# A decoder layer's recurrence: key transposes moved from TensorE to VectorE squares and transfers within SBUF

## The chip, the cores and the metric

One Trainium2 chip, one NeuronCore. The metric is the device time of the whole program in microseconds (us), the median of several runs.

## What is computed

A hybrid decoder layer on 256 tokens of width 2048, in float32. Its first part is a mixer with two branches, mLSTM and RWKV-7. The change touches the RWKV branch alone: 16 heads of size 64, a state matrix per head that goes from token to token.

```python
def step(state, inp):
    rt, wt, kt, vt, kkt, kat = inp
    state = (state * wt[:, :, None, :]
             - jnp.einsum('bhvk,bhk->bhv', state, kkt)[..., None] * kat[:, :, None, :]
             + vt[..., None] * kt[:, :, None, :])
    return state, jnp.einsum('bhvk,bhk->bhv', state, rt)
```

Around it stand projections by large weight matrices (some 350 MB of weights in all), cross-attention and a gated feed-forward.

## The kernel before, in words

Nearly all of TensorE's time goes to products of weights with activations. Each float32 product is made of three passes of a shorter float type: weight-high by activation-high, weight-high by activation-low and weight-low by activation-high. A weight comes from HBM in chunks of 512 KB (tile `raw`, four buffers; `Feed.dma`, line 384, issued on SP's queue at L392). ScalarE makes the high part (`wh`, L414) and VectorE the low part (`wl`, L458); both have four buffers. While TensorE works on chunk i, the program asks for the high and low parts up to chunk i+3 and for loads up to chunk i+6 (lines 545 and 546). A chunk is 24 matmuls of 256 columns (`fm`) or 12 of 512 (`tm`).

Everything else is woven between these products by `Spread` (line 71). Tasks are Python generators. `half()` runs at half-chunk steps, and a task with `chain=n` is given one piece (up to its next `yield`) every n such steps. `need(task)` runs a task to its end at once. This fixes the order in which each engine's instructions are written; each engine then works through its own list strictly in order, and waits at an instruction until what it reads is there and what it overwrites has been read. SP's queue is such a list too. The tile framework gives the queue's transfers eight completion semaphores in rotation, so a transfer can also wait for the one eight places ahead of it.

The RWKV recurrence (`rwkv`, line 1116, a chain task with a piece at every third step) works in four chunks of 64 tokens. `BK` holds the scaled keys with features on partitions, `[128, 8, 4, 2, 64]`: eight pairs of heads, four chunks, two kinds of key, 64 tokens. For chunk c it makes X, a two-level triangular solve (`lv1`, `lv2`), U, and, for chunks 0 to 2, the update `Tn` of the state. `Tn` needs the keys with tokens on partitions (`bkt`, in tile `bg`). `turn` (line 1155) makes them: TensorE transposes eight 128x128 squares per chunk into PSUM, two with `lv1`, two with `lv2` and four before U, and ScalarE copies them to `bg` (lines 1197, 1227 and 1250). The mLSTM branch (`mlstm`, line 1386) runs in the same stretch: products `den` and `num` on TensorE, then a chain of small steps over ScalarE (`rd`, `jk`), VectorE (`rd`, `var`, `rh`, `so`) and GpSimd (`rh`), for each of the two halves of the tokens.

The tile `gr2` `[128, 2, 1024]` has a second half that the solve of the inverses used (`L`, line 1036) and that is free once the recurrence begins.

Of the kernel before, what the change touches and what calls it, by code (L numbers as in the profile page):

```python
# [15 lines left out]
P = 128  # L16
# [129 lines left out]
def _layer(ctx, tc, nc, d, dbg):  # L146
    act, dve = Meter(nc.scalar, 200.0, 0.83), Meter(nc.vector, 70.0, 1.04)
    pool, pe, sp = nc.gpsimd, nc.tensor, nc.sync
    side = Spread(act, dve)
# [18 lines left out]
    def C(name, tag, shape=None, dt=F32):  # L168
        return mp.tile(shape or [P, S], dt, tag=tag, bufs=1, name=name)
# [7 lines left out]
    def aux(name, shape=None):  # L177
        return pp.tile(shape or [P, 512], F32, tag="aux", bufs=4, name=name)

    def mm(out, lhsT, rhs, start=True, stop=True):  # L180
        pe.matmul(out, lhsT, rhs, start=start, stop=stop, skip_group_check=True)  # L181
# [20 lines left out]
    def ccol(n, w, o=0):  # L202
        return con[:, CC[n] + o:CC[n] + o + w]

    ident = ccol("id", 128)
# [36 lines left out]
    def bc(ap, n):  # L242
        return ap.unsqueeze(1).broadcast_to((ap.shape[0], n, ap.shape[1]))
# [440 lines left out]
    M, tasks = {}, {}  # L684
# [424 lines left out]
            yield  # L1109


    T = [cp.tile([P, 4, 64], F32, name=f"T{hf}") for hf in range(2)]

    GAP = 3

    def rwkv():
        KR, BK, vt, cmt = M["KR"], M["BK"], M["vt"], M["cmt"]
        sm, im = ccol("sm", 64), ccol("im", 64)
        flat = lambda ap: ap.rearrange("p a t -> p (a t)")
# [2 lines left out]
        heads = [(hf, j, e) for hf in H for j in range(4) for e in H]  # L1122
        bg = C("bg", "bg0", [P, 2, 512])
        bkt = [bg[:, hf].rearrange("p (j t) -> p j t", j=4) for hf in H]
        gr = M["gr"]
        ab, uv = M["ab"], [v[:, 1] for v in M["au"]]
        m0, m1 = M["m0"], C("m", "m1", [P, 2, 4, 32])
# [4 lines left out]
        def gram(c, hf):  # L1132
            qs = [aux("gram", [P, 4, 128]) for _ in H]
            for j in range(4):
                for e in H:
                    mm(qs[e][:, j], flat(BK[E2[e], hf * 4 + j, c]), flat(KR[E2[e], hf * 4 + j, c]))

            def evac():
                for e in H:
                    dve.tensor_mul(ab[c][hf][:, e], qs[e][:, :, 0:64], bc(sm, 4))  # L1140
                    dve.tensor_mul(gr[hf][c % 2][:, e], qs[e][:, :, 64:128], bc(im, 4))
            return evac

        def early(c):
            def mask():
                for hf in H:
                    v = gr[hf][c].rearrange("p e j t -> p (e j) t")
                    nc.vector.tensor_mul(v, v, bc(im, 8))
                dve.spent += 1345.0
            return mask  # L1150
# [1 line left out]
        def booked():  # L1152
            dve.spent += 1345.0

        def turn(q, c, hf, js):
            for j in js:
                pe.transpose(q[:, j - js[0]], flat(BK[:, hf * 4 + j, c]), ident)

        def inverse(c, hf, k):
            return cmt[:, k, :, c * 8 + hf * 4:c * 8 + hf * 4 + 4].rearrange("p s j -> p j s")  # L1160

        def diagonal(c):
            for hf in H:
                dve.tensor_copy(m0[:, hf], inverse(c, hf, 0))
# [12 lines left out]
        def carried(c):  # L1177
            for hf in H:
                for e in H:
                    act.copy(ab[c][hf][E2[e], e], KR[E2[e], hf * 4:hf * 4 + 4, c, 0])  # L1180
                    act.copy(uv[hf][E2[e], e], T[hf][E2[e]])

        def quarter(name, c, js, more):
            q = aux(name, [P, 512])
            if more:
                turn(q[:, 256:512].rearrange("p (j t) -> p j t", j=2), c, 1, js)
            return q, q[:, 0:256].rearrange("p (h j s) -> p h j s", h=2, j=4)

        def level1(c, q, v, more):
            for hf, j, e in heads:  # L1190
                mm(v[quart[1][e], hf, j], ab[c][hf][quart[0][e], e, j, 32:64], m0[quart[0][e], hf, j])

            def evac():
                act.copy(m1[quart[1][0]], v[quart[1][0]])
                dve.tensor_copy(m1[quart[1][1]], v[quart[1][1]])
                if more:
                    act.copy(flat(bkt[1][:, 0:2]), q[:, 256:512])
            return evac

        dve.spent += 350.0  # L1200
        transposed(0)
        values(0)
        yield
        level1(0, *quarter("lv1", 0, (0, 1), True), True)()
        yield
        for c in range(4):
            more = c < 3

            if c % 2 == 0:
                ysb = [C(f"ysb{hf}", f"ysb{hf}", [P, 8, 64]) for hf in H]  # L1210
            q, v = quarter("lv2", c, (2, 3), more)
            x = aux("X", [P, 2, 4, 64])
            for hf, j, e in heads:
                r = slice(0, P) if c else E2[1 - e]
                mm(x[E2[e], hf, j], ab[c][hf][r, e, j], uv[hf][r, e, j])
            ev = []
            if more:
                ev.append(gram(c + 1, 0) if c == 2 else booked if c else early(0))
            for hf, j, e in heads:
                mm(v[quart[0][e], hf, j], m1[quart[1][e], hf, j], mt[hf][quart[1][e], j, 32:64])  # L1220
            for hf in H:
                for e in H:
                    r = quart[0][e]
                    dve.tensor_copy(mt[hf][r, :, 32:64], v[r, hf])
                    act.copy(uv[hf][E2[e], e], x[E2[e], hf])
            if more:
                act.copy(flat(bkt[1][:, 2:4]), q[:, 256:512])
            for f in ev:
                f()
            yield  # L1230
            if more:
                diagonal(c + 1)
            yield

            if c == 2:
                yield from turned(0, ysb_done)
                yield
            q = aux("U", [P, 2, 4, 64])
            ev = []
            if more:  # L1240
                qb = aux("bkt", [P, 4, 128])
                turn(qb, c, 0, (0, 1, 2, 3))
                ev.append(gram(c + 1, 1) if c == 2 else booked if c else early(1))
            for hf, j, e in heads:
                mm(q[E2[e], hf, j], mt[hf][E2[e], j], uv[hf][E2[e], e, j])
            for hf in H:
                act.copy(uv[hf][E2[0], 0], q[E2[0], hf])
                dve.tensor_copy(uv[hf][E2[1], 1], q[E2[1], hf])
            if more:
                act.copy(bkt[0], qb)  # L1250
            for f in ev:
                f()
            yield
            if more:
                transposed(c + 1)
            yield

            if more:
                lv1 = quarter("lv1", c + 1, (0, 1), c + 1 < 3)
                q = aux("Tn", [P, 2, 4, 64])  # L1260
                for hf, j, e in heads:
                    mm(q[E2[e], hf, j], bkt[hf][:, j, e * 64:e * 64 + 64], uv[hf][:, e, j])
            qy = aux("Y", [P, 2, 4, 64])
            for hf, j, e in heads:
                mm(qy[E2[e], hf, j], gr[hf][c % 2][:, e, j], uv[hf][:, e, j], start=(hf == 0 and j == 0), stop=(c == 0))
            if c:
                for hf, j, e in heads:
                    mm(qy[E2[e], hf, j], KR[E2[e], hf * 4 + j, c, 1], T[hf][E2[e], j], start=False)
            f = level1(c + 1, *lv1, c + 1 < 3) if more else None
            if more:  # L1270
                for hf in H:
                    pcb = pce[:, hf * 4:hf * 4 + 4, c].unsqueeze(2).broadcast_to((P, 4, 64))
                    if c:
                        dve.tensor_add(T[hf], T[hf], q[:, hf])
                        dve.tensor_mul(T[hf], T[hf], pcb)
                    else:
                        dve.tensor_mul(T[hf], q[:, hf], pcb)
            cr = E2[c % 2]
            for hf in H:
                ye = ysb[hf].rearrange("p (a b) v -> p b a v", b=2)  # L1280
                for e in H:
                    act.copy(ye[cr, e], qy[E2[e], hf])
            if c == 0:
                for hf in H:
                    nc.vector.tensor_mul(gr[hf][0].rearrange("p e j t -> p (e j) t"),
                                         M["gr2"][:, 0, hf * 512:hf * 512 + 512].rearrange("p (a t) -> p a t", a=8), bc(im, 8))
            if f:
                f()
            yield
            if more:  # L1290
                values(c + 1)
                yield
                carried(c + 1)
            yield
            if c % 2:
                ysb_done = ysb
                yield from norm(ysb, [gr[hf][1].rearrange("p e j t -> p (e j) t") for hf in H])
# [798 lines left out]
def _ptile(v):  # L2096
    return np.ascontiguousarray(v.reshape(-1, P).T)

# [83 lines left out]
```

## Time and profile before

| | |
|---|---|
| median of 3 runs | 1858.66 us (1858.31 to 1858.88) |
| profiled execution, its own time | 1858.71 us |
| span of the profile, first to last instruction | 1856.9 us |
| TensorE busy | 1848.2 us, 100% of the span |
| VectorE, ScalarE, GpSimd busy | 70%, 55%, 2% |
| chain of work that ended last, TensorE's share | 96% |

The span is 1.8 us shorter than the execution's own time. A busy share is the time in which at least one instruction of an engine runs; matmuls overlap, so TensorE at 100% says that it is never left without work, not that it works at its peak. The chain is followed back from the last instruction to whatever released it; its shares say which engine's work the end waited for. The recurrence lies between 295 and 475 us from the span's start.

### The profile page before, as it was taken

To read this page: it belongs to the slowest core of one execution; us is meant where nothing else is said; L and a number is where in the kernel's file an instruction comes from. 1 tells how busy PE (TensorE), PEld (TensorE's weight loads), DVE (VectorE), ACT (ScalarE), POOL (GpSimd) and SP (SyncE) were. 2 spreads that over 40 slices of the span, in tenths; PEclk is the share of its full clock that TensorE was granted. 3 is DMA by queue.
4 is the path that set the end of the run, shared out by engine and by line. 5 is a ranking of instruction groups with operands and counts; after the bars stand their busy time and mean duration, and the time that the engine had idled before them with its cause. 6 is when DMAs were issued, how large, how long until landed. Compare 5 with 4: busy or idle time off the path is not lost.

```text
span 1856.9 us, 36219 instructions
## 1 busy us (share of the span) xinstructions
PE 1848.2 (100%) x14902; PEld 1763.8 (95%) x14902; DVE 1302.8 (70%) x1857; ACT 1013.1 (55%) x1492; POOL 35.2 (2%) x64
## 2 busy tenths in 40 slices
PE   9999999999999999999999999999999999999998
PEld 9999888999999999999999999999999988888887
DVE  7789787566676857787876677766666775556565
ACT  7776445655454746666544555444445554555544
POOL 0100020000000000000000000000000000000000
PEclk9999999999999999999999999999999999999999
DMA  8556544455556765455776666666666666666664
GB/s 276 182 175 194 181 152 161 131 166 155 178 193 196 272 203 181 163 178 180 214 226 200 194 197 187 193 197 197 196 193 194 193 194 216 192 193 193 194 192 145
DMA packets 100454, 353.56 MB, mean 190 GB/s; under 512 B 11520, under 2 KB 12800, under 8 KB 99904
## 3 DMA queue, kind: packets, MB, share of 16 engines
q1 hardware_dynamic: 99712, 350.33, 59.8%
q8 instruction: 116, 1.90, 0.4%
q10 hardware_dynamic: 576, 0.92, 0.2%
q14 instruction: 50, 0.41, 0.1%
HBM read 347.01 MB, written 2.10 MB: 188 GB/s over the span
## 4 chain that ended last, share of the span: by engine, by line
PE 96%; DVE 1%; DMA 1%; ACT 0%; issue 0%; SPq 0%; DVEq 0%; ACTq 0%
PE fm L181 67%; PE tm L181 25%; DMA w<-in_w_in_dram 1%; DVE wl L458 0%; PE gram L181 0%; PE Y L181 0%; PE num L181 0%; PE lv L181 0%; DVE ql L66 0%; PE X L181 0%; PE U L181 0%; PE zg L181 0%; PE zwa L181 0%; DVE z L66 0%; DVE stx L66 0%
## 5 line engine op out<-in xcount | busy, mean ns | idle before, releaser
L458 DVE TENSOR_TENSOR wl<-raw,wh 128x1024 fp32r<-128x1024 f32 x639 | 775.4, 1218 | 405.6 <-ACT wh L414 401.2
L414 ACT CAST wh<-raw 128x1024 fp32r<-128x1024 f32 x639 | 664.6, 1045 | 485.7 <-PE fm L181 371.7
L181 PE MATMUL fm<-fh,wh 128*128 128x256 f32 x2048 | 563.8, 276 | 0.6 <-DVE fh L66 0.6
L181 PE MATMUL fm<-fh,wl 128*128 128x256 f32 x2048 | 563.5, 276 | 0.0
L181 PE MATMUL fm<-fl,wh 128*128 128x256 f32 x2048 | 563.4, 276 | 0.0
L181 PEld LDWEIGHTS fm<-fh,wh 128*128 128x128 f32 x2048 | 383.7, 188 | 0.8 <-DVE fh L66 0.8
L181 PEld LDWEIGHTS fm<-fl,wh 128*128 128x128 f32 x2048 | 383.6, 188 | 0.0
L181 PEld LDWEIGHTS fm<-fh,wl 128*128 128x128 f32 x2048 | 383.6, 188 | 0.0
L181 PE MATMUL tm<-wh,as 128*128 128x512 f32 x1024 | 315.2, 389 | 0.0
L181 PE MATMUL fm<-hh,wh 128*128 128x256 f32 x1024 | 283.8, 279 | 0.0
L181 PE MATMUL fm<-hh,wl 128*128 128x256 f32 x1024 | 281.5, 277 | 0.0
L181 PE MATMUL fm<-hl,wh 128*128 128x256 f32 x1024 | 281.3, 277 | 0.0
L181 PEld LDWEIGHTS tm<-wh,as 128*128 128x128 f32 x1024 | 192.1, 188 | 39.7
L181 PE MATMUL tm<-wl,as 128*128 128x512 f32 x512 | 199.2, 389 | 0.0
L181 PEld LDWEIGHTS fm<-hh,wh 128*128 128x128 f32 x1024 | 192.1, 188 | 0.7 <-ACT hh L66 0.2
L181 PEld LDWEIGHTS fm<-hl,wh 128*128 128x128 f32 x1024 | 191.5, 188 | 0.1
L181 PEld LDWEIGHTS fm<-hh,wl 128*128 128x128 f32 x1024 | 191.4, 188 | 0.0
L181 PEld LDWEIGHTS tm<-wl,as 128*128 128x128 f32 x512 | 96.1, 188 | 20.2
L66 ACT CAST as<-ac 128x256 fp32r<-128x256 f32 x128 | 45.6, 404 | 110.8 <-PE tm L181 110.8
L66 DVE TENSOR_TENSOR as<-ac,as 128x256 fp32r<-128x256 f32 x128 | 48.5, 421 | 61.7 <-ACT as L66 61.7
L181 PE MATMUL fm<-mgh,wh 128*128 128x256 f32 x256 | 70.9, 277 | 0.0
L181 PE MATMUL fm<-mgl,wh 128*128 128x256 f32 x256 | 70.8, 276 | 0.0
(417 smaller groups left out, 2218.9 us busy)
## 6 DMA issues: line engine op xcount, KB each, us to landing
raw<-in_w_fu_dram SPq DMA_DIRECT2D x256, 512.0 KB, 4.2
raw<-in_w_in_dram SPq DMA_DIRECT2D x154, 512.0 KB, 3.6
raw<-in_w_fd_dram SPq DMA_DIRECT2D x128, 512.0 KB, 3.9
raw<-in_w_br_dram SPq DMA_DIRECT2D x32, 512.0 KB, 3.9
raw<-in_w_mo_dram SPq DMA_DIRECT2D x32, 512.0 KB, 3.9
raw<-in_w_xk_dram SPq DMA_DIRECT2D x8, 512.0 KB, 4.2
raw<-in_w_xv_dram SPq DMA_DIRECT2D x8, 512.0 KB, 3.6
raw<-in_w_xq_dram SPq DMA_DIRECT2D x8, 512.0 KB, 3.8
```

The lines of the kernel that those rows point to most:

```text
L66: return f(out, *a, **k)
L181: pe.matmul(out, lhsT, rhs, start=start, stop=stop, skip_group_check=True)
L414: nc.scalar.copy(wh[:, v], r[:, v])
L458: nc.vector.tensor_sub(wl[:, v], r[:, v], self.st[self.nl][0][:, v])
```

## The change

A new chain task, `keys_turn`, gets the keys of chunks 0, 1 and 2 into token order inside `BK` itself. Per chunk VectorE transposes 32x32 squares, with two instructions of 128x512 elements, from `BK` into the free half of `gr2`. Then 16 transfers on SP's queue, each 32 partitions by 2 rows of 512 bytes, carry the squares to their places over `BK`'s chunk. The task is given a piece at every half-chunk step (`chain=1`), whatever the engines' budgets (`free=True`), and `need(tasks["keys"])` writes out what is left of it before U of chunk 0. The 24 TensorE transposes go. ScalarE's copies to `bg` stay, with the same number of elements, but read `BK` in SBUF. The planner's budgets are booked as if nothing had changed.

```diff
+    def keys_turn():
+        sq = M["gr2"][:, 1].rearrange("p (q k e) -> p k q e", q=4, k=8)
+        for c in range(3):
+            v = M["BK"][:, :, c].rearrange("p k b t -> p k (b t)")
+            for h in range(2):
+                h4 = slice(h * 4, h * 4 + 4)
+                nc.vector.transpose(sq[:, h4], v[:, h4].rearrange("p k (q s) -> p k q s", q=4))
+                yield
+            yield
+            for q in range(4):
+                for f in range(4):
+                    sp.dma_start(v[q * 32:q * 32 + 32, f * 2:f * 2 + 2],
+                                 M["gr2"][f * 32:f * 32 + 32, 1, q * 256:q * 256 + 256].rearrange("p (h i) -> p h i", h=2))
+            yield
...
+        tasks["keys"] = side.add(keys_turn(), chain=1, free=True)
...
-        def turn(q, c, hf, js):
-            for j in js:
-                pe.transpose(q[:, j - js[0]], flat(BK[:, hf * 4 + j, c]), ident)
+        def turn(c, hf, js):
+            src = BK[:, :, c].rearrange("p (f h) b t -> p h f (b t)", h=2)[:, hf]
+            src = src.rearrange("p f (j w) -> p j f w", j=4)
+            act.copy(bkt[hf][:, js].rearrange("p j (f w) -> p j f w", f=4), src[:, js])
...
+            if c == 0:
+                side.need(tasks["keys"])
...
-                qb = aux("bkt", [P, 4, 128])
-                turn(qb, c, 0, (0, 1, 2, 3))
...
-                act.copy(bkt[0], qb)
+                turn(c, 0, slice(0, 4))
+                if c == 0:
+                    turn(c, 1, slice(0, 4))
```

In the order of instructions three places matter. First VectorE's list at chunk 0 of the recurrence. Before, the low weight parts (`wl`) and the copies out of `lv1` and `lv2` (to `m` and `mt`) follow one another:

```order
L66 TENSOR_TENSOR mt_3575<-cmt_3004,con_73 128x256 [waits DVE_49]
L66 TENSOR_TENSOR mt_3576<-cmt_3004,con_73 128x256
L458 TENSOR_TENSOR wl_3591<-raw_3529,wh_3589 128x2x512 [waits DMAHW4_49,PE_49,Activation_49]
L66 COPY m_3574<-lv1_3607 32x256 [waits Activation_49]
L458 TENSOR_TENSOR wl_3631<-raw_3547,wh_3629 128x1024 [waits DMAHW5_49,DVE_49,Activation_49]
L458 TENSOR_TENSOR wl_3649<-raw_3565,wh_3647 128x1024 [waits DVE_49,DMAHW6_49,PE_49,Activation_49]
L66 COPY mt_3575<-lv2_3661 32x4x32 [waits DVE_49,PE_49]
```

After the change, the part of the list from the first transpose of key chunk 1 to `pws`, the first step of the mLSTM's second half (`DMAHW0` to `DMAHW7` are the eight semaphores of SP's transfers):

```order
L1118 STREAM_TRANSPOSE gr2_3119<-BK_1316 128x4x4x32 [waits DMAHW4_49,DMAHW3_49,DMAHW5_49,DMAHW2_49,DMAHW6_49,DMAHW1_49,DMAHW7_49,DMAHW0_49,DVE_49]
L458 TENSOR_TENSOR wl_3665<-raw_3565,wh_3663 128x1024 [waits PE_49,Activation_49]
L66 COPY mt_3575<-lv2_3677 32x4x32 [waits PE_49]
L66 COPY mt_3575<-lv2_3677 32x4x32
L66 COPY mt_3576<-lv2_3677 32x4x32 x2
L1164 TENSOR_TENSOR gx_2996<-gx_2996,con_73 128x512
L1164 TENSOR_TENSOR gx_2997<-gx_2997,con_73 128x512
L1118 STREAM_TRANSPOSE gr2_3119<-BK_1316 128x4x4x32 [waits DVE_49]
L458 TENSOR_TENSOR wl_3732<-raw_3594,wh_3730 128x1024 [waits PE_49,Activation_49]
L66 COPY m_3521<-cmt_3004 128x128 x2
L1118 STREAM_TRANSPOSE gr2_3119<-BK_1316 128x4x4x32 [waits DMAHW4_49,DMAHW3_49,DMAHW5_49,DMAHW2_49,DMAHW6_49,DMAHW1_49,DMAHW7_49,DMAHW0_49,DVE_49]
L1118 STREAM_TRANSPOSE gr2_3119<-BK_1316 128x4x4x32 [waits DVE_49]
```

Six transposes came in; the third and the fifth wait for all transfers of the chunk before, since they overwrite the squares that these read, and `wl`, `mt` and later `pws` stand behind them.

Second, SP's list in the same stretch, as the difference between the two:

```order
-L392 DMA raw<-in_w_in_dram 128x1024 x103
+L392 DMA raw<-in_w_in_dram 128x1024 x92
+L1123 DMA BK<-gr_3119 32x2x128 x16
+L392 DMA raw<-in_w_in_dram 128x1024 x2
+L1123 DMA BK<-gr_3119 32x2x128 x32
+L392 DMA raw<-in_w_in_dram 128x1024 x9
```

Between 92 and 103 weight loads 48 transfers of keys came in, with two weight loads between the first 16 and the other 32.

Third, TensorE at `lv1` of chunk 0, as the difference:

```order
 L181 MATMUL tm<-wl,hh 128x512
-L1157 MATMUL lv_3607<-con,BK 128x128 x2
-L181 MATMUL lv_3607<-m,ab 32x32 x16
+L181 MATMUL lv_3609<-m,ab 32x32 x16
 L181 MATMUL tm<-wh,hh 128x512
```

The two transposes are gone and nothing else moved.

## Rows read from the trace of the kernel before

**Rows 1.** The page: busy time and share of each engine; the chain's shares by engine.
```profile
PE 1848.2 (100%) x14902; PEld 1763.8 (95%) x14902; DVE 1302.8 (70%) x1857; ACT 1013.1 (55%) x1492; POOL 35.2 (2%) x64
...
PE 96%; DVE 1%; DMA 1%; ACT 0%; issue 0%; SPq 0%; DVEq 0%; ACTq 0%
```

**Rows 2.** Windows: stretch, length, PE, PEld, DVE, ACT, POOL busy; PE clock, DMA share, GB/s.
```profile
295.00:328.00 33.00, 33.00 (x317) 29.73 (x317) 21.39 (x38) 17.16 (x38) 1.02 (x1) 1.00 0.49 161
...
1850.00:1857.00 7.00, 1.29 (x5) 0.68 (x4) 2.67 (x4) 1.66 (x6) 0.00 (x0) 0.87 0.54 201
```

**Rows 3.** Chain of work that ended last, in order of time: start, us, what.
```profile
299.99 0.22 PE lv L1157 x2
...
318.30 0.44 PE bkt L1157 x4
...
340.64 9.63 PE fm L181 x84
```

**Rows 4.** The transposes' line, L1157: count, duration ns min/median/max, first and last start.
```profile
L1157 PE MATMUL lv<-con,BK x12: 270/272/273, 299.8 to 404.3; 128*128 128x128 f32 x12
...
L1157 PE MATMUL bkt<-con,BK x12: 270/272/273, 318.1 to 425.0; 128*128 128x128 f32 x12
```

**Rows 5.** Timeline of PE, 318 to 329 us: start, us, what.
```profile
318.14 0.60 PE L1157 MATMUL bkt<-con,BK 128*128 128x128 f32 x4
318.67 1.15 PE L181 MATMUL U<-au,mt 64*64 64x64 f32 x32
...
323.96 0.95 PE L181 MATMUL den<-ones,pws 128*128 128x1 f32 x8
324.76 3.70 PE L181 MATMUL num<-vm,pw 128*128 128x256 f32 x16
328.11 0.47 PE L181 MATMUL fm<-hh,wh 128*128 128x256 f32 x1
```

**Rows 6.** VectorE's transposes of squares, groups by line: busy us, mean ns of one.
```profile
L1063 DVE STREAM_TRANSPOSE cmt<-gr 128x1024 f32<-128x1024 f32 x1 | 2.1, 2108 | 0.0
...
L66 DVE STREAM_TRANSPOSE cmt<-gr 128x1024 f32<-128x1024 f32 x1 | 1.2, 1233 | 0.0
...
L1994 DVE STREAM_TRANSPOSE xsq<-xr 128x256 f32<-128x256 f32 x16 | 7.0, 437 | 0.0
```

**Rows 7.** Timeline of SP's queue near 900 us: four transfers within SBUF, then a weight load.
```profile
901.48 2.46 SPq L1997 DMA_DIRECT2D xt<-xsq  x4
904.04 6.67 SPq L392 DMA_DIRECT2D raw<-in_w_fu_dram  x4
```

**Rows 8.** Line L1997, transfers within SBUF: issue ns min/median/max, and time to landing.
```profile
L1997 SPq DMA_DIRECT2D xt<-xsq x32: 512/586/674, 901.5 to 978.1; - x32
...
DMA to landing us min/median/max: 2.5/3.7/4.5
```

**Rows 9.** Line L392, weight loads: issue ns min/median/max, and time to landing.
```profile
L392 SPq DMA_DIRECT2D raw<-in_w_in_dram x154: 327/328/1102, 14.1 to 573.9; - x154
...
DMA to landing us min/median/max: 2.7/4.0/11.4
```

**Rows 10.** SP's own waits, 285 to 340 us: us in total, times, longest.
```profile
SPq L392 <- DVE wl L458: 43.6, 12, 9.1
```

**Rows 11.** Timeline of VectorE, 297 to 319 us.
```profile
297.41 1.16 DVE L66 TENSOR_TENSOR mt<-cmt,con 128x256 f32<-128x256 f32 x2
298.50 1.21 DVE L458 TENSOR_TENSOR wl<-raw,wh 128x1024 fp32r<-128x1024 f32 x1
...
307.13 1.18 DVE L66 COPY mt<-lv 32x128 f32<-32x128 f32 x4 [1.17 <-PE lv L181]
308.34 1.29 DVE L1148 TENSOR_TENSOR gx<-gx,con 128x512 f32<-128x512 f32 x2
...
311.30 0.68 DVE L66 TENSOR_TENSOR pws<-pw 128x512 f32<-128x512 f32 x1
...
316.70 1.66 DVE L66 SCALAR_TENSOR_TENSOR so<-num,rh,so 128x256 f32<-128x256 f32 x4
```

**Rows 12.** Timeline of ScalarE: the first `jk` of the mLSTM's first half.
```profile
313.23 0.47 ACT L66 ACTIVATE jk<-num,rd 128x256 f32<-128x256 f32 x1 [0.80 <-PE num L181]
```

More of the change, by code (lines that the diff above doesn't have):

```diff
@@ L1181, in carried, with quarter, level1 @@
                     act.copy(uv[hf][E2[e], e], T[hf][E2[e]])
[L1183 to L1189, printed above, removed]
+        def quarter(name):
+            return aux(name, [P, 2, 4, 32])
+        def level1(c, v, more):
             for hf, j, e in heads:
@@ L1195, in evac @@
                 dve.tensor_copy(m1[quart[1][1]], v[quart[1][1]])
-                if more:
-                    act.copy(flat(bkt[1][:, 0:2]), q[:, 256:512])
+                if more and c:
+                    turn(c, 1, slice(0, 2))
+                elif more:
+                    act.spent += act.fixed + act.per * 256
             return evac
@@ L1203, in rwkv @@
         yield
-        level1(0, *quarter("lv1", 0, (0, 1), True), True)()
+        level1(0, quarter("lv1"), True)()
         yield
@@ L1210, in rwkv @@
                 ysb = [C(f"ysb{hf}", f"ysb{hf}", [P, 8, 64]) for hf in H]
-            q, v = quarter("lv2", c, (2, 3), more)
+            v = quarter("lv2")
             x = aux("X", [P, 2, 4, 64])
@@ L1225, in rwkv @@
                     act.copy(uv[hf][E2[e], e], x[E2[e], hf])
-            if more:
-                act.copy(flat(bkt[1][:, 2:4]), q[:, 256:512])
+            if more and c:
+                turn(c, 1, slice(2, 4))
+            elif more:
+                act.spent += act.fixed + act.per * 256
             for f in ev:
@@ L1258, in rwkv @@
             if more:
-                lv1 = quarter("lv1", c + 1, (0, 1), c + 1 < 3)
+                lv1 = quarter("lv1")
                 q = aux("Tn", [P, 2, 4, 64])
@@ L1268, in rwkv @@
                     mm(qy[E2[e], hf, j], KR[E2[e], hf * 4 + j, c, 1], T[hf][E2[e], j], start=False)
-            f = level1(c + 1, *lv1, c + 1 < 3) if more else None
+            f = level1(c + 1, lv1, c + 1 < 3) if more else None
             if more:
```

## The prediction

> **What bounds the kernel now.** I read the page's busy shares first, then its chain. TensorE is busy for the whole span and 96% of the chain is TensorE's work, while VectorE has 30% idle [rows 1]. The same holds where the change acts: from 295 to 328 us TensorE is busy for all 33 us, VectorE for 21.4 and ScalarE for 17.2, and the transfer engines are half used [rows 2]. So an instruction taken from TensorE shortens the run by what it occupies there, and work added on VectorE or on SP's queue is free as long as nothing that TensorE reads comes late through it. The question is therefore what stands behind the new waits in those two lists.
>
> **What the removal gives.** 24 transposes go, 12 with `lv` and 12 for `bkt` [rows 4]. Each is 272 ns long but overlaps the next: the chain gives 0.22 us to two and 0.44 to four [rows 3], 0.11 each, so 24 x 0.11 = 2.64 us. From start to start four of them and the step to U take 0.53 us [rows 5], which would make 24 x 0.13 = 3.2 us; that is the upper end. I take 2.64, all of it on the path. ScalarE's copies keep their element count and only change their source; ScalarE is idle half the time here [rows 2], so I cost them at nothing. The lost cover would be a ScalarE that is late with `wh`.
>
> **What a chunk's 16 transfers take.** The nearest rows are the transfers within SBUF near 900 us, also 32 partitions each. Four are issued in 2.46 us and the next load starts 2.56 us after the first [rows 7], 0.64 us from one to the next; one lands 3.7 us after its issue [rows 8]. So from the first issue to the last landing I put b = 15 x 0.64 + 3.7 = 13.3 us. The low end takes the issue of a weight load, 0.33 us [rows 9], and the quickest landing, 2.5 [rows 8]: 15 x 0.33 + 2.5 = 7.5. The high end takes the longest issue, 0.67 [rows 8], with the same gap of 0.05, and the slowest landing, 4.5: 15 x 0.72 + 4.5 = 15.3. I stay with 13.3, since those rows are of the same kind of transfer, from the same queue, in a row.
>
> [...] The rows have 0.64 in a series. [...]
>
> **The new waits, step by step.** A new transpose has 512 elements: twice the 437 ns of the 256-element ones [rows 6] is 0.87 us, with 0.62 and 1.05 (half of the two 1024-element ones) as ends. Times are on the clock of the profile of before.
> - VectorE is through with `mt` at 298.5 [rows 11]. Transpose 0a, one `wl` of 1.21, transpose 0b: 301.45. Then SP issues chunk 0's transfers, landed at 301.45 + b = 314.75.
> - Transpose 1a overwrites the squares that these transfers read, so VectorE stands still at it until then, and behind it `wl` (1.21), the `mt` copies (1.18), `gx` (1.29) [rows 11], then 1b: 0.87 + 1.21 + 1.18 + 1.29 + 0.87 = 5.42 more, so 306.87 + b = 320.2. In the profile before, U, which needs these `mt`, starts at 318.67 [rows 5] and `mt` was ready at 308.3; now it is ready at 318.0 on a TensorE that is by then 0.9 us earlier (8 transposes). That is at its limit; a wait of about a microsecond here vanishes in the longer one that follows.
> - SP issues chunk 1's transfers after 1b; they land at 306.87 + 2b = 333.5. Transposes 2a and 2b, one after the other, wait for that: 308.61 + 2b = 335.2.
> - Behind them stands `pws`, which `den` of the mLSTM's second half reads. TensorE came to `den` at 323.96 [rows 5], so here it stands from about 323 on. After `pws` come `rd`, ScalarE's `jk`, `var`, GpSimd's power, `rh` and `so`. From `pws` to the end of `so` took 311.30 to 318.36 [rows 11], 7.06 us, with some 0.9 us in it in which `jk` waited for TensorE's `num` [rows 12]; without that 6.2. The second `num` reuses the PSUM that `so` reads and needs half of the four `so`: 5.5 us after 2b. `num` then takes 324.76 to 328.11, 3.35 us [rows 5].
> - So `num` ends at 308.61 + 2b + 5.5 + 3.35 = 317.46 + 2b, where it ended at 328.11: 2b - 10.65 later. The other 16 transposes give 1.76 back afterwards. **Net: 2b - 12.4 = +14.2 us** at b = 13.3, +2.6 at 7.5, +18.2 at 15.3.
>
> The weights do not add to it. `wl` of the next chunks follows `so` while `num` runs. The first weight load behind all 48 transfers goes out at 335.2 + 16 x 0.64 = 345.4, lands 4.0 us later [rows 9], and is ready after a cast and a subtraction of some 2.3 us at 351.7. TensorE reads it at 340.64 [rows 3] plus 15.7, the shift at that point, at 356.3. The added VectorE work itself, 6 x 0.87 = 5.2 us, fits in its idle time. Chunk 2's transfers are first read a chunk of the recurrence later.
>
> **The clock.** TensorE would stand for over 10 us with little between. [...] I put 2 us, with 0 and 4 as ends. [...]
>
> **The sum.** The profiled execution took 1858.71 us (its span 1856.9 and 1.8 around it), 0.05 from the median of the runs. 1858.7 + 14.2 + 2 = 1874.9, so **1875 us**.
>
> **The rivals.**
> - *The transfers are quick enough, and the run is not slower.* Net is zero loss, -2.64, where 2b - 12.4 = -2.64, so for b of 4.9 us or less: 1856.1 us (1855.5 at the upper end of the removal). For it speaks only that 16 transfers of 32 KB are as many bytes as one weight load; against it that even at the issue of a weight load, 0.33 us each, 15 issues take 5 us before the last begins to move. Between 4.9 and 8 us the loss and the gain are within 3.7 us of each other, at about 1859: this is the case at the low end of b.
> - *SP's queue starves the weights.* SP issues in order; its own waits here, 43.6 us for `wl` [rows 10], are what a full queue of weights looks like. With 32 key transfers and no load between them, a pace p per issue delays the first load to 308.61 + 2b + 16p, and ready to 6.3 us after it, against a need at 340.64 + 2b - 10.65 - 0.2: it decides from p = 0.93 us on. If the two rows of 512 bytes per partition make an issue cost twice, p = 1.28: b = 22.9, net +33.4, then 5.6 for weights and 2 for the clock: 1900 us.
>
> **How the numbers follow.** A measurement of this kernel can tell about 0.2%, 3.7 us, from no change. The forecast's mechanism with b between 8 and 15.3 us: 0.82. The low end of b, within 0.2% of before: 0.08. Quick transfers: 0.03, of which a third beyond 0.2% if waits of the old run go too. Starved weights or an issue still longer: 0.07. So faster 0.02, same 0.09, slower 0.89. The range goes from b = 7.5 without a clock loss, 1861, less 1 for shorter transposes, to b = 15.3 with 4 us of clock, 1881, plus 1 for longer ones: 1860 to 1882.
>
> **What would show it.** In the profile of the changed kernel: no line of transposes on TensorE; two waits of VectorE at the new transposes, of about 10 us each, released by transfers; TensorE idle by some 10 us before `den` and again before `num` near 324 to 341, and busy elsewhere; 16 issues in about 10 us on SP's queue, three times; a granted clock below 1.00 after the gap. Wrong would be: a TensorE that stays at 100% near 330 us (then b is under 8), transfers that land as one batch within 5 us, or idle time of TensorE that ends at `wl` or `wh` for weights that landed late.

## The result and the profile after

The changed kernel takes 1874.63 us (median of 4 runs, 1874.29 to 1875.12) against 1858.49 of the kernel before on the same chip: a ratio of 1.0087, 95% interval 1.0071 to 1.0103. It is 16.1 us slower; the forecast was 1875. The profiled execution took 1874.46 us with a span of 1872.6.

The page of the changed kernel, busy shares and the shares of the chain that ended last:

```profile
PE 1850.2 (99%) x14878; PEld 1765.2 (94%) x14878; DVE 1306.7 (70%) x1863; ACT 1013.3 (54%) x1491; POOL 35.2 (2%) x64
...
PE 98%; SPq 1%; DVE 1%; ACT 0%; issue 0%; DMA 0%; POOL 0%; DVEq 0%; ACTq 0%; POOLq 0%
```

Against [rows 1] TensorE has 24 instructions less and VectorE 6 more, and 1% of the chain now lies on SP's queue, all of it between 320 and 340 us. Windows of that stretch (columns as in [rows 2]):

```profile
295.00:328.00 33.00, 28.01 (x285) 24.93 (x283) 13.65 (x21) 9.12 (x17) 0.00 (x0) 0.98 0.42 125
328.00:345.00 17.00, 9.35 (x46) 8.47 (x47) 10.12 (x19) 6.52 (x16) 1.02 (x1) 0.63 0.22 57
345.00:360.00 15.00, 13.35 (x190) 13.05 (x189) 10.57 (x22) 10.88 (x26) 1.01 (x1) 1.00 0.62 226
```

TensorE was busy for all of the first stretch before [rows 2]; now it is idle for 5.0, 7.65 and 1.65 us of the three, 14.3 in all, and its mean granted clock is 0.63 in the second. What it waits for stands in its timeline (start, us, what, idle time before and what ended it):

```profile
332.76 1.86 PE L181 MATMUL den<-ones,pws 128*128 128x1 f32 x8 [9.75 <-DVE pws L66]
337.51 5.19 PE L181 MATMUL num<-vm,pw 128*128 128x256 f32 x16 [2.88 <-DVE so L66]
346.76 1.15 PE L181 MATMUL Tn<-au,bg 128*64 128x64 f32 x32
350.50 0.69 PE L181 MATMUL lv<-m,ab 32*32 32x32 f32 x32 [1.65 <-DVE so L66]
...
355.33 1.04 PE L1449 MATMUL haT<-con,so 128*128 128x128 f32 x8
```

In the kernel before `Tn` and `lv` started at:

```profile
332.75 1.15 PE L181 MATMUL Tn<-au,bg 128*64 128x64 f32 x32
334.77 0.69 PE L181 MATMUL lv<-m,ab 32*32 32x32 f32 x32
```

Each time it is VectorE that is late, with `pws`, with `so` of the mLSTM's first half and with `so` of its second half (`lv` is the first level of the solve for the recurrence's chunk 1). VectorE's timeline says why:

```profile
298.17 0.71 DVE L1118 STREAM_TRANSPOSE gr<-BK 128x512 f32<-128x512 f32 x1
299.90 0.71 DVE L1118 STREAM_TRANSPOSE gr<-BK 128x512 f32<-128x512 f32 x1
312.97 0.71 DVE L1118 STREAM_TRANSPOSE gr<-BK 128x512 f32<-128x512 f32 x1 [9.95 <-DMA BK<-gr]
317.29 0.71 DVE L1118 STREAM_TRANSPOSE gr<-BK 128x512 f32<-128x512 f32 x1
330.83 1.31 DVE L1118 STREAM_TRANSPOSE gr<-BK 128x512 f32<-128x512 f32 x2 [11.32 <-DMA BK<-gr]
332.06 0.65 DVE L66 TENSOR_TENSOR pws<-pw 128x512 f32<-128x512 f32 x1
336.58 1.66 DVE L66 SCALAR_TENSOR_TENSOR so<-num,rh,so 128x256 f32<-128x256 f32 x4
349.56 1.66 DVE L66 SCALAR_TENSOR_TENSOR so<-num,rh,so 128x256 f32<-128x256 f32 x4
```

It stands still for 9.95 and 11.32 us at the two transposes that overwrite squares still being read, and `pws` comes right behind the second. What it waits for stands on SP's queue:

```profile
300.70 10.88 SPq L1123 DMA_DIRECT2D BK<-gr  x16
311.68 3.47 SPq L392 DMA_DIRECT2D raw<-in_w_in_dram  x2
318.06 24.47 SPq L1123 DMA_DIRECT2D BK<-gr  x32
```

and the transfers' line over the whole run (issue ns min/median/max, then the time to landing):

```profile
L1123 SPq DMA_DIRECT2D BK<-gr x48: 585/594/1467, 300.7 to 341.9; - x48
...
DMA to landing us min/median/max: 1.8/1.9/4.2
```

From the first issue to VectorE's next transpose are 312.97 - 300.70 = 12.3 us for chunk 0 and 330.83 - 318.06 = 12.8 for chunk 1. For chunk 0 that is the 10.88 us of its 16 issues and one landing.

### The profile page after: what moved, and what is told of

Same layout as the page of the kernel before. It is cut to its first block, busy times and chain, and to the rows that moved or that the text cites. A ratio compares the mean times of both kernels' runs of the same rounds, so it can differ in the third digit from the quotient of the medians.

```text
span 1872.6 us, 36242 instructions
## 1 busy us (share of the span) xinstructions
PE 1850.2 (99%) x14878; PEld 1765.2 (94%) x14878; DVE 1306.7 (70%) x1863; ACT 1013.3 (54%) x1491; POOL 35.2 (2%) x64
## 4 chain that ended last, share of the span: by engine, by line
PE 98%; SPq 1%; DVE 1%; ACT 0%; issue 0%; DMA 0%; POOL 0%; DVEq 0%; ACTq 0%; POOLq 0%
PE fm L181 68%; PE tm L181 25%; SPq L1123 1%; PE gram L181 0%; PE Y L181 0%; PE lv L181 0%; PE U L181 0%; PE X L181 0%; PE zg L181 0%; PE zwa L181 0%; DMA BK<-gr 0%; PE stb L181 0%; PE warm L181 0%; PE xsc L181 0%; PE xo L181 0%
```

## The experiments

The runs were made in three groups (1 to 4; 5, 6, 7 and 9; 8, 10 and 11), each beside the kernel before on the same chip, whose median was 1858.66, 1859.0 and 1858.65 us. The theory to be tried, A: the whole loss is VectorE standing in order behind 16 issues in a row. For the rivals the first question was what is left when the waits go. In the quoted expectations "the paced kernel" is run 2 and "the spread kernel" run 9.

**1. The removal alone.** Edit: the task is not started, so the keys stay unturned (this kernel is for its time alone).

```diff
-        tasks["keys"] = side.add(keys_turn(), chain=1, free=True)
...
-            if c == 0:
-                side.need(tasks["keys"])
```

> Leaves out the turning of the keys altogether: no TensorE transposes, no VectorE squares, no transfers; ScalarE's copies read the keys unturned. What is left of the change is the removal of 24 transposes from TensorE and ScalarE's copies from SBUF. Theory A (the loss is VectorE's stand behind the 16 issues of a chunk, the gain is 24 x 0.11 = 2.64 us): 1855.3 to 1856.1 us, against 1858.5 of the kernel before. Rival D (the copies from SBUF, or the order of PSUM buffers without the bkt tiles, cost something of their own): above 1856.5, up to 1858.5.

Measured: 1857.07 us (11 runs), ratio 0.9992 [0.9984, 1.0001]. The removal gave 1.6 us by the medians, where 2.4 to 3.2 were expected: a miss of theory A, inside the range of rival D. The interval is wide enough to hold 2.64, so the two profiles were laid side by side by the starts of the same instructions on TensorE. From X of chunk 0 to U of chunk 1 twelve transposes went, and 1.2 us are gained, 0.10 each, as priced. Then, between U of chunk 1 and X of chunk 2 (362 to 404 us), 0.9 of it is given back, though four more transposes went there, with no gap of TensorE to be seen. The matmuls of the weights (`fm`) in a window of 20 us there, in the kernel before:

```profile
380.00:400.00 20.00, 20.00 (x179) 20.00 (x178) 1.38 (x2) 0.00 (x0) 1.00 0.49 159
```

and in this one:

```profile
380.00:400.00 20.00, 20.00 (x172) 20.00 (x172) 1.38 (x2) 0.00 (x0) 1.00 0.54 155
```

Both are busy throughout at a granted clock of 1.00, and yet one runs 179 matmuls in it and the other 172: 4% fewer. From start to start they stand 113.3 ns apart in the kernel before and 117.8 ns here. That was in nobody's theory; runs 10 and 11 take it up. They keep the copies from SBUF and the order of PSUM buffers, which rival D held to blame, and are 2.2 and 2.3 us below the kernel before; so these are not shown to cost anything.

**2. All parts, but apart.** Chunk 1's squares and transfers are written out after U of chunk 0, chunk 2's after U of chunk 1; ScalarE's copies all stand at U.

```diff
-    def keys_turn():
+    def keys_turn(c):
...
-        for c in range(3):
...
+            if c < 2:
+                tasks["keys", c + 1] = side.add(keys_turn(c + 1), chain=1, free=True)
```

> All parts of the change stay, 48 transfers on SP's queue included, but chunk 1's squares and transfers are written out only after U of chunk 0, and chunk 2's after U of chunk 1, each far from the one before, so that no transpose waits for transfers of the chunk before. Theory A: no wait of VectorE at the transposes, no idle TensorE near 325 to 350, clock 1.00, so 1855.3 to 1857.0 us, below the kernel before. Rival B (48 transfers on SP's queue delay the weight loads or crowd the transfer engines, wherever they stand): 1862 or more, since they are all still there. Rival C (the clock fell for another reason than the gap): a granted clock below 1.00 here too.

Measured: 1857.58 us (11 runs), ratio 0.9994 [0.9985, 1.0004], 0.6 above what was expected. No transpose waits for a transfer and the clock is 1.00. So 48 transfers on SP's queue, six transposes on VectorE and the copies from SBUF cost nothing near 16 us: rival B falls, and so does rival C's other reason for the clock. But the transfers are not quite free. SP's queue at chunk 2:

```profile
371.75 10.73 SPq L1122 DMA_DIRECT2D BK<-gr  x16
382.58 7.98 SPq L392 DMA_DIRECT2D raw<-in_w_in_dram  x5
```

and the waits from 380 to 410 us:

```profile
ACT wh L414 <- DMA raw<-in_w_in_dram: 3.1, 1, 3.1
...
PE fm L181 <- DVE wl L458: 0.4, 1, 0.4
```

Behind 16 issues in a row a weight is late; by 402 us TensorE is 0.9 us later against the kernel before than at 396.

**3. Only the first of the two waits.** Chunks 0 and 1 as in the changed kernel, chunk 2 after U of chunk 1.

```diff
-        tasks["keys"] = side.add(keys_turn(), chain=1, free=True)
+        tasks["keys"] = side.add(keys_turn((0, 1)), chain=1, free=True)
...
+            if c == 1:
+                tasks["keys"] = side.add(keys_turn((2,)), chain=1, free=True)
```

> Takes away only the second of the two waits of VectorE: chunks 0 and 1 are turned as in the changed kernel, so the transposes of chunk 1 still wait some 10 us for chunk 0's transfers; chunk 2 is turned after U of chunk 1. Theory A (the first wait is covered by work that TensorE has ahead, only the second, with pws behind it, reaches TensorE): 1855.3 to 1858 us. Rival C (both waits cost alike, about half of the loss each): about 1865.

Measured: 1863.4 us (6 runs, 1861.84 to 1865.83), ratio 1.0027 [1.0015, 1.0038]. A miss of theory A as it stood, since the first wait is not covered, and nearer to rival C, though the two waits do not cost alike. It is 5.8 us above the paced kernel. The waits, in a profiled execution that took 1865.01 us:

```profile
DVE gr L1118 <- DMA BK<-gr: 9.7, 1, 9.7
...
PE lv L181 <- DVE so L66: 3.1, 1, 3.1
...
PE num L181 <- DVE so L66: 0.9, 1, 0.9
```

`den` waits for nothing here, so up to there the 9.7 us are absorbed. But VectorE does not catch up: its `so` of the second half is at 336.75 where the kernel before has it at 331.10, and `lv` of chunk 1 waits for that. `lv` starts at 337.68 us, 2.9 after the kernel before, and the low clock that follows this gap (0.74 on the mean of 339 to 343 us) adds some 1.5 by 344 us. The second wait adds the remaining 1874.6 - 1863.4 = 11.2 us, as much as its whole length of 11.3. Of the first wait some 6 us are lost, of the second as much as all: this reads as a slack of VectorE that is used up once. No run has the second wait without the first, so that last step is argued.

**4. The same transfers from GpSimd's queue.**

```diff
-                    sp.dma_start(v[q * 32:q * 32 + 32, f * 2:f * 2 + 2],
+                    pool.dma_start(v[q * 32:q * 32 + 32, f * 2:f * 2 + 2],
```

> The changed kernel with its 48 transfers issued on GpSimd's queue instead of SP's; both waits of VectorE stay. Theory A: the wait is set by 16 issues in a row and one landing; if GpSimd issues one in the 0.64 us that SP takes, VectorE waits 20 to 24 us as before and the run takes 1872 to 1877 us; with an issue of 1 us or more it is 1885 or more. Rival B (the loss comes from transfers standing between weight loads on SP's queue): about 1857, since SP's queue then has weight loads alone.

Measured: 1878.5 us (4 runs), ratio 1.0108 [1.0094, 1.0122]. SP's queue has weight loads alone, and the loss is still there, so rival B falls a second time. The waits show the old one and a new one:

```profile
DVE gr L1118 <- DMA BK<-gr: 19.2, 2, 10.0
...
PE num L181 <- DVE so L66: 9.0, 1, 9.0
DVE rh L66 <- POOL rh L228: 8.4, 2, 7.2
```

GpSimd issues in 0.53 us but with pauses of 0.16 to 0.80 us within a chunk, so VectorE waits for nearly as long (19.2 us for 21.3), and GpSimd's own `rh`, a link of the mLSTM's chain, stands behind chunk 2's issues until 340.19 us. TensorE's three waits together are 2.8 us longer than in the changed kernel, which nobody had expected and which puts the time 1.5 us above the expected range.

**5. Half the issues on each queue.**

```diff
-                    sp.dma_start(v[q * 32:q * 32 + 32, f * 2:f * 2 + 2],
+                    (sp if f < 2 else pool).dma_start(v[q * 32:q * 32 + 32, f * 2:f * 2 + 2],
```

> The changed kernel with half of a chunk's 16 transfers issued on SP's queue and half on GpSimd's, side by side; both waits of VectorE stay, the same 48 transfers move the same bytes. Theory A (the loss is the number of issues in a row on one queue): 8 issues of 0.64 us and a landing of 1.9 us make 6.4 us from the first issue to the last landing, or up to 8 with GpSimd's pauses; by the prediction's formula, with b = 6.4 to 8, 0.4 to 3.6 us more than the kernel before, so 1858 to 1863 us with what is left of the last wait. Rival (the bytes or the transfer engines set the time): 1872 or more, as the changed kernel.

Measured: 1868.21 us (4 runs), ratio 1.0049 [1.0035, 1.0062]. The two series of 8 ran side by side (5.4 us on SP's queue, 4.4 on GpSimd's), and VectorE's waits went from 21.3 to 13.6 us:

```profile
DVE gr L1118 <- DMA BK<-gr: 7.0, 1, 7.0
DVE gr L1118 <- DMA raw<-in_w_in_dram: 6.6, 1, 6.6
...
PE num L181 <- DVE so L66: 5.3, 1, 5.3
```

(The profile puts the second of these lines down to a weight load; it is the wait of chunk 1's first transpose, on chunk 0's transfers. Whether a load held it for a part of the time is not known.) The same bytes with half the issues on each queue shorten the wait, so the rival falls: it is the issues in a row on one queue. The time missed its expectation by 5 us: from the first issue to the next transpose were 309.45 - 300.48 = 9.0 and 322.90 - 314.49 = 8.4 us, not 6.4 to 8, and the longer wait before `num` is again `rh` on GpSimd behind its own issues (VectorE waits 2.7 us for it, 1.1 in other runs).

**6. Twice the issues.** Each transfer is split into two of one row.

```diff
+                    for h in range(2):
+                        sp.dma_start(v[q * 32:q * 32 + 32, f * 2 + h],
+                                     M["gr2"][f * 32:f * 32 + 32, 1, q * 256 + h * 128:q * 256 + h * 128 + 128])
```

> The changed kernel with each transfer split into two of one row of 512 bytes per partition: twice the issues, the same bytes. Theory A: b = 31 x 0.64 + 1.9 = 21.7 us, twice more than 12.5 in the sum, so 1874.6 + 18.4 = 1893 us, and up to 1899 with weight loads that now come late behind 64 issues without a load between them. Rival (bytes): 1875.

Measured: 1898.65 us (2 runs), ratio 1.0213 [1.0195, 1.0232], 24 us above the changed kernel with the same bytes and at the upper end of what theory A allowed. The waits:

```profile
DVE gr L1118 <- DMA BK<-gr: 38.1, 2, 19.2
PE den L181 <- DVE pws L66: 17.6, 1, 17.6
ACT wh L414 <- DMA raw<-in_w_in_dram: 9.3, 2, 9.0
PE fm L181 <- DVE wl L458: 7.4, 1, 7.4
PE haT L1450 <- ACT ysb L66: 4.9, 1, 4.9
```

VectorE's waits grow by 16.8 us, and the first of them now reaches TensorE by itself, 7.4 us through `wl`. Here the prediction's second rival is seen as well: behind 64 issues without a load ScalarE waits 9.0 us for a weight, and TensorE 4.9 for ScalarE.

**7 and 8. TensorE kept busy in its gaps.** Small matmuls of constants into `den`'s PSUM tile, before `den` and before `num` of the second half; in run 7 each `mm` made two instructions, so the filler ran twice as long as meant.

```diff
+            for _ in range(88 if t else 0):
+                mm(qd[:, 4:4 + P], ones.broadcast_to((P, P)), ones.broadcast_to((P, P)))
...
+            for _ in range(26 if t else 0):
+                mm(qd[:, 4:4 + P], ones.broadcast_to((P, P)), ones.broadcast_to((P, P)))
```

> The changed kernel with 114 small matmuls of constants (88 before den of the mLSTM's second half, 26 before num, 128 columns each), so that TensorE works through the 9.8 and 2.9 us in which it stood idle there; the waits of VectorE and what they release stay as they are. The granted clock stays 1.00 from 325 to 345 us. Theory A (the clock costs some 2 us of the loss: num took 5.2 us instead of 3.7, and what follows ran slow up to 340.6): 1872.0 to 1873.3 us, against 1874.6 of the changed kernel. Rival: what runs at the low clock is hidden by the wait for so, and nothing is won: 1874.3 or more.

Measured: 1882.4 us (4 runs), 1.0126 [1.0111, 1.0142]. The filler itself held `den` up (to 342.6 us, with `pws` ready at 332.6), so the run decides nothing about the clock's price. Run 8 has 43 and 12 in the place of 88 and 26:

> As the run before with small matmuls in TensorE's idle time, which held twice as many instructions as meant (176 and 52 of 0.11 us, 19.8 and 6.0 us): now 86 before den and 24 before num of the mLSTM's second half, 9.7 and 2.7 us, so that den and num start when VectorE lets them. Theory A (the clock costs some 2 us of the loss): granted clock 1.00 throughout, 1872.0 to 1873.3 us. Rival (what ran slow was hidden by the wait for so): 1874.3 or more.

Measured: 1876.12 us (4 runs), 1.0095 [1.0081, 1.0109]. Not faster; the rival holds. TensorE's timeline in this run:

```profile
332.99 1.05 PE L181 MATMUL den<-ones,pws 128*128 128x1 f32 x8
...
337.73 3.72 PE L181 MATMUL num<-vm,pw 128*128 128x256 f32 x16 [0.91 <-DVE so L66]
345.56 1.15 PE L181 MATMUL Tn<-au,bg 128*64 128x64 f32 x32
350.70 0.69 PE L181 MATMUL lv<-m,ab 32*32 32x32 f32 x32 [3.06 <-DVE so L66]
...
357.15 1.04 PE L1453 MATMUL haT<-con,so 128*128 128x128 f32 x8
```

The granted clock is 1.00 through `num`, which takes 3.72 us instead of 5.19, and `Tn` starts 1.2 us earlier than in the changed kernel. All of it is lost at `lv`, which waits for VectorE's `so` and starts at 350.70, where it started at 350.50. So up to `lv` the low clock of the changed kernel cost nothing. And the clock, kept up so far, falls after this longer gap: 0.57 on the mean of 351 to 355 us, 1.00 there in the changed kernel. There no other wait hides it: from `lv` to `haT` it takes 6.45 us instead of 4.83, and these 1.6 us are about what this run is slower than the changed kernel.

**9. Transfers four at a time.** The paced kernel with a yield after every four transfers (the edit against run 2).

```diff
         for q in range(4):
             for f in range(4):
                 sp.dma_start(...)
-        yield
+            yield
```

> The paced kernel with the 16 transfers of a chunk issued four at a time at successive half-chunk steps, so that weight loads stand between them on SP's queue. In the paced kernel TensorE lost 0.9 us near 396 to 402 us, where a weight came late behind 16 key transfers in a row. Theory: that loss goes, no wait takes its place: 1856.3 to 1857.2 us, at least 1.3 us below the kernel before. Rival (the transfers cost what they cost wherever they stand): as the paced kernel, 1857.6 or more.

Measured: 1857.48 us (11 runs), 0.9992 [0.9983, 1.0001]. The wait for the late weight is gone, TensorE has no gap over 0.15 us in the recurrence; in the profiles the stretch from X of chunk 0 to X of chunk 2 takes 98.84 us, as with the removal alone, against 99.52 in the paced kernel and 99.16 in the kernel before. The medians cannot tell it from the paced kernel; 1857.48 is 0.3 above what was expected, and 1.5 below the kernel before. Between 380 and 400 us it has 172 matmuls, as the removal alone.

**10 and 11. The pace.** One transpose on TensorE before U of chunk 1, its result overwritten by U; then four.

```diff
             q = aux("U", [P, 2, 4, 64])
+            for j in range(1 if c == 1 else 0):
+                pe.transpose(q.rearrange("p a b s -> p (a b s)")[:, j * 128:j * 128 + 128], flat(BK[:, j, c]), ident)
```

> The spread kernel with one transpose of a 128x128 square, whose result is overwritten, on TensorE before U of chunk 1. Between U of chunk 1 and X of chunk 2 (some 362 to 404 us) every kernel without the transposes issues its fm matmuls 117.8 ns apart, the kernel before 113.3 ns apart, at the same granted clock; that is 0.85 us of what the removal should have given. Theory P (the pace is kept by TensorE from one group to the next, and the transposes before U had set the quicker one): 113.3 ns from there on, X of chunk 2 some 0.7 us earlier, 1856.5 to 1857.2 us in all. Rival Q (the pace comes from the transfers or from the other engines at that time): 117.8 ns, 1857.5 or more.

> The same with four such transposes before U of chunk 1, as many as the kernel before has there. Theory P, if one is not enough: 113.3 ns between U of chunk 1 and X of chunk 2, and the 0.45 us of the four transposes lost: 1856.8 to 1857.5 us. Rival Q: 117.8 ns as in the spread kernel, 1857.9.

Measured: 1856.48 us with one, 0.9990 [0.9981, 0.9999], and 1856.34 with four, 0.9989 [0.9980, 0.9998] (11 runs each); with four that is 0.5 below what was expected. The window of run 1, with one transpose:

```profile
380.00:400.00 20.00, 20.00 (x179) 20.00 (x178) 1.38 (x2) 0.00 (x0) 1.00 0.56 172
```

179 matmuls again, with all the transfers and squares in place. From X of chunk 0 to X of chunk 2 it takes 97.86 us in the profile, 1.0 less than the spread kernel; the medians cannot tell the two apart.

But the transposes are not shown to set the pace. The expectation of run 10 says that every kernel without them runs at 117.8 ns there; of those already run, two do not. The last 20 us of weights before X of chunk 2 in run 4 and in run 6, which have no transposes there:

```profile
404.00:424.00 20.00, 20.00 (x179) 20.00 (x178) 1.38 (x2) 0.00 (x0) 1.00 0.56 159
```

```profile
424.00:444.00 20.00, 20.00 (x179) 20.00 (x178) 1.38 (x2) 0.00 (x0) 1.00 0.51 159
```

And in run 2 the pace goes from 117.8 to 113.3 ns at the late weight near 395 us, again without a transpose. With one transpose the `fm` right behind U stay at 117.8, and the quicker pace begins only behind `lv`, near 376 us, as in runs 4 and 6; so the one transpose need have nothing to do with it. With four, as in the kernel before, the quicker pace begins right behind U, and in no run without them does it. Theory P is left for that stretch alone, and what sets the pace is open. The four transposes cost no measurable time. Both of these kernels are 0.1% below the kernel before, with intervals that end just short of 1. Runs 2, 9, 10 and 11 are forms of the change that lose nothing.

## Why the prediction was right

**The mechanism, and the formula 2b - 12.4.** The mechanism is right. The two waits stand at the transposes named, of about the length named (9.95 and 11.32 for "about 10 us each"), released by transfers, and runs 2, 5 and 6 show that they go, shrink and grow with the number of issues in a row at the same bytes. The formula falls short: with the two b of the trace, 12.3 and 12.8, it gives 12.7 us, where 16.1 were lost. It ends at `num`, and the path did not (see the gap, below).

**b = 15 x 0.64 + 3.7 = 13.3 us.** It was 12.3 and 12.8, over-sized by 0.5 to 1. The pace held, with 594 ns of issue at the median for the 586 of [rows 8], but one issue in each of the first two series took over a microsecond (1.11 and 1.47), so chunk 0's 16 took 10.88 us instead of 10.3. The landing was over-sized: 1.9 us at the median where the transfers near 900 us had 3.7 [rows 8]. Those are not quite the same kind: they move 64 KB each, these 32.

**The transpose of 512 elements, 0.87 us.** It took 0.71, so nearer to the low end; in run 2 the six of them have no effect of their own that could be seen.

**"The weights do not add to it."** Right: TensorE's three waits end at `pws` and `so`, none at `wl`. With twice the issues, in run 6, a weight is late by 9.0 us.

**The gap, piece by piece.** The first wait before `den` came as 9.75 us. "Again" some 10 before `num` was a slip against the prediction's own steps, which have 5.5 us from the second transpose to `num` with `den` in between; 2.88 were idle. A third wait, 1.65 us before `lv`, was not predicted at all. That is the failed step, an omission: the first half's chain from `pws` to `so` was followed up to `num`, while the second half's `rd`, `jk`, `rh` and `so` behind it on VectorE were not, though `lv` of chunk 1 waits for them. Run 8 shows what it is worth, 3.06 us of idle time before `lv` once `num` runs at the full clock, and run 3 has the same 3.06 us after a wait that `den` doesn't feel. (The profile's chain also passes through seven issues of chunk 2 on the way to this `so`, by ScalarE's copy to `bg` at 341.3 us. That copy does not wait for them: in run 6 it starts at 358.17, while chunk 2's issues go on to 369.8.)

**The clock, +2 us.** It fell as said, to 0.50 between 327 and 339 us, after TensorE had been idle from 323 us, and `num` took 5.19 us for 3.70 [rows 5]. But the price was wrongly put. The 2 us were the author's estimate, and no run shows them: run 8 took the low clock away from `num` and won nothing, since `lv` waits for VectorE's `so` whatever `num` does. From the start of `pws` to `lv` the two kernels take 18.4 us alike. So the term of 2 us came to nothing here. Behind `lv`, where nothing hides it, a low clock cost 1.6 us in run 8 and some 1.5 in run 3; in the changed kernel the clock was back by then.

**The removal, 24 x 0.11 = 2.64.** The price of a transpose was right, but the run then goes through some 40 us at a pace 4% slower, and the net is the 1.6 us of run 1. The term was over-sized by 1 us. (Run 11, with the quicker pace and 20 transposes less, gained 2.3 by the medians, where 20 x 0.11 is 2.2.)

**Why the sum came out all the same.** Partly by luck. By its own steps the run should have been 2 x 13.3 - 10.65 + 2 - 0.2 = 17.7 us behind at `lv` of chunk 1 (two more transposes are gone there). In the profiles it was 350.50 - 334.77 = 15.7. `pws` came at 332.06, 3.1 us before the 335.2 of the prediction (the two b, the first issue at 300.70 for 301.45, shorter transposes); the clock's 2 us were not paid; and the 3.1 us of the chain that was left out came on top: -3.1 - 2 + 3.1 = -2.0. Behind `lv` 14 more transposes should have given 1.5 back, and nothing came back: the spans end 1872.6 - 1856.9 = 15.7 us apart. So the forecast loss of 16.2 us met 15.7 in the profiles, and 16.1 by the medians, because errors of 2 to 3 us cancelled. Counted the other way: TensorE is idle for 14.3 us and busy for 3.2 us more than in run 1 (1850.2 against 1847.0), of which `den` and `num`, 0.9 and 1.5 us longer than before [rows 5], are most; less the 1.6 of run 1 that makes 15.9.

**The rivals.** That the transfers are quick enough needed b of 4.9; even with two queues it was 8.4 to 9.0. That SP's queue starves the weights did not come about here, did so mildly in run 2 (0.9 us) and plainly in run 6.

**The chances.** A third of 0.03 is 0.01, so by its own reasons the prediction had faster at 0.01 and same at 0.10; nothing hangs on it.

## What to carry to other kernels

On VectorE an instruction that waited for transfers (9.95 and 11.32 us) held up what stood behind it, `wl`, `mt` and `pws` among it; where a change puts such a wait into an engine's list, ask how long the series of issues is, what slack the engine has, and what else stands behind. Here the first of two such waits lost some 6 of its 9.7 us, the second as much as its whole length. The same work, written out with distance between a buffer's reuse and its transfers (run 2), lost none of the 16 us. Follow the chain to the last instruction that shares the late engine, not to the first one that waits.

## What the runs showed of the hardware

- TensorE ran the same 256-column matmuls, busy throughout and at a granted clock of 1.00, at 113.3 ns or at 117.8 ns from start to start, for tens of microseconds; over 20 us that is 179 matmuls or 172. In the last 20 us before X of chunk 2 the kernel before and runs 4, 6, 10 and 11 have the quicker pace, the changed kernel and runs 1, 5, 7, 8 and 9 the slower one. What sets it is not known.
- A transfer of 32 partitions by two rows within SBUF took 0.59 us of SP's queue and 0.53 of GpSimd's; on SP's, one issue of the first sixteen and one of the second took 1.11 and 1.47 us. Halving the bytes of each (run 6) left the issue at 0.59 us.
- The granted clock. In the changed kernel it was at 0.50 while TensorE stood or worked in short pieces between 327 and 339 us, and back at 1.00 from 343 on; it stayed there after the idle 1.65 us before `lv`:

```profile
327.00:331.00 4.00, 0.00 (x0) 0.00 (x0) 0.17 (x1) 0.00 (x0) 0.00 (x0) 0.50 0.16 41
331.00:335.00 4.00, 1.86 (x8) 1.78 (x8) 1.96 (x5) 1.89 (x9) 0.00 (x0) 0.50 0.10 26
335.00:339.00 4.00, 1.49 (x4) 1.22 (x5) 2.75 (x7) 2.18 (x4) 1.02 (x1) 0.50 0.20 50
...
351.00:355.00 4.00, 4.00 (x46) 3.96 (x41) 4.00 (x7) 3.35 (x7) 0.00 (x0) 1.00 0.39 118
```

In run 8, after the idle 3.06 us before `lv`, it fell with a delay, when TensorE was busy again:

```profile
347.00:351.00 4.00, 0.94 (x41) 0.81 (x38) 1.56 (x6) 3.48 (x9) 1.01 (x1) 1.00 0.88 359
351.00:355.00 4.00, 4.00 (x44) 3.96 (x37) 4.00 (x8) 3.06 (x8) 0.00 (x0) 0.57 0.36 111
```
